# Prompt attention's scores, maxima and exponentials issued two turns ahead of the value products instead of one

## The chip, the cores and the metric

The kernel runs on one core of one Trainium2 chip. A core has five engines that work side by side, each with its own list of instructions and each waiting on semaphores for the others: TensorE (PE: matmuls, with its weight loads as PEld), VectorE (DVE), ScalarE (ACT), GpSimd (POOL, here mostly gathers by index) and SyncE (SP, which issues transfers). Matmul results land in PSUM banks and are read from there by DVE or ACT. The metric is the device time of one execution in microseconds (us); lower is better.

## The reference

One inference step of a hybrid decoder layer, for 512 prompt tokens and 8 samples of 4 new tokens each (their past is 4096 positions in a paged cache). The layer is a feed-forward block, a mixer of a gated linear recurrence (HGRN2, 4 heads) and a latent softmax attention (MLA, 4 heads), and a second feed-forward block:

```python
def layer(h, ...):
    h = h + 0.5 * rmsnorm(swiglu(rmsnorm(h, norm_g[0]), wg[0], wu[0], wd[0]), norm_g[1])
    m, c_kv, k_r, s_fin = mixer(rmsnorm(h, norm_g[2]), ...)
    h = h + rmsnorm(m, norm_g[3])
    h = h + 0.5 * rmsnorm(swiglu(rmsnorm(h, norm_g[4]), wg[1], wu[1], wd[1]), norm_g[5])

def mixer(u, ...):
    z = u @ w_in                        # columns for both head groups
    ...                                 # o_h: the recurrence's output
    qh = jnp.einsum('btc,chd->bthd', cq, w_q_up)
    ...                                 # rotary parts q_r, k_r; latent rows c_kv
    o_lat = mla_attend(q_lat, q_r, keys_c, keys_r, pos, k_pos)
    o_m = jnp.einsum('bthr,rhv->bthv', o_lat, w_uv)
    o = jnp.concatenate([o_h..., o_m...], axis=-1)
    return o @ w_out, c_kv, k_r, s_fin

def mla_attend(...):                    # per block of 128 queries
    s = (einsum('bqhr,bsr->bhqs', ql, c_kv) + einsum('bqhd,bsd->bhqs', qr, k_rope)) * scale
    s = jnp.where(k_pos <= q_pos, s, -jnp.inf)
    p = jax.nn.softmax(s, axis=-1)
    return einsum('bhqs,bsr->bqhr', p, c_kv)
```

## The kernel before

The 544 tokens are held with the features on the partitions and the tokens along the free axis, in two parts: part 0 is the prompt's first 256 tokens (tiles whose names end in a), part 1 the other 256 prompt tokens and the 32 sample tokens (names ending in b). Every large product is split in a high and a low part (`wh`/`wl`, `uha`/`ula`, `PTh`/`PTl`), three matmuls for one.

Around the change the program has these steps. A **turn** of the prompt attention is one pair (head, part); there are eight, `heads`: heads 0 to 3 of part 0, then heads 0 to 3 of part 1. A turn has these pieces.

- `prep(hd)`: the query projection of one head, 36 matmuls (line 259) on a weight tile split by ACT (`wh`, line 250) and DVE (`wl`, line 251), then scaled by DVE (lines 1158 to 1160) and split into `qnh` and `qnl`.
- `soft(hd, x)`: scores of two blocks of 128 queries on PE (lines 1188 and 1190), of 128 and 256 keys for part 0 and of 384 and 512 for part 1; the row maximum on DVE (1195, 1196), the exponential on ACT (1199), the division by the row sum on DVE (1200, 1201). The result is the tile `pe`.
- `latent(hd)`: the samples' latent query (1170, copied by ACT at 1171).
- `value(hd, x, pes)`: `pe` is transposed on PE (1211), split into `PTh` (ACT, 170) and `PTl` (DVE, 171), multiplied with the values (1220), and the sum `o` copied by ACT into `ma` or `mb` (1222).

The loop over turns is the code in which the changed number stands:

```python
PJ = (0, 0, 0, 0, 4, 4, 2, 1)
DP = 6
PJ0, LOOK = 4, 1
...
            for hd in range(LOOK):
                prep(hd)
            pe_ = [soft(*heads[i]) for i in range(LOOK)]
            for i, (hd, x) in enumerate(heads):
                if i + LOOK < len(heads):
                    if i + LOOK < NH:
                        prep(i + LOOK)
                    else:
                        qsplit_n(i + LOOK - NH, 1, qnb[:, i + LOOK - NH])
                    pe_.append(soft(*heads[i + LOOK]))
                ...
                value(hd, x, pe_[i])
```

From turn 4 (`PJ0`) on, the output projection of part 0, `project(0, ...)`, is woven in: eight products with `w_o` of 24 matmuls each, 4 in turn 4, 4 in turn 5; each is copied by ACT (770), squared (298), scaled (301), and the squares added by DVE (300). Its sum of squares `ssp` goes through PE (191) and two ACT steps (`rs_t` 197, `s_post` 198), and DVE then scales and adds (312, 313) before ACT and DVE split the second feed-forward block's input (207, 208). The first products of that block (line 277, steps of the generator `gb`) start there. `decode_prep` and `qsplit` copy the samples' queries into place (1229, 1231, 1238), and after the loop the sample decode begins, whose gathers (POOL, 1352 and 1359) use the slots of the prompt keys: `ulb`, `uhb`, `ha`, `hb`.

The written order isn't the executed one. A planner puts each engine's instructions in a fixed order; instructions that could go earlier are put between others, as long as data and buffers allow. PSUM tiles made with `ps(...)` come from four banks in rotation (`CYC`), so that a tile waits until the one made four before it has been read.

Of the kernel before, what the change touches and what calls it, by code (L numbers as in the profile page):

```python
# [47 lines left out]
PJ = (0, 0, 0, 0, 4, 4, 2, 1)  # L48
DP = 6
LAG, BEG = 2, 0  # L50
PJ0, LOOK = 4, 1
W1 = (5, 7)
NPS, PRT = {"ps": 2, "po": 1, "pm": 1, "acc": 4}, "ps"
CYC = ("ps", "po", "ps", "pm")
# [1640 lines left out]
```

## Time and profile before

| | |
|---|---|
| time of three runs | 1250.42 us median (1248.77 to 1251.25) |
| the profiled execution's own time | 1257.12 us |
| its span, first to last instruction | 1255.3 us |
| mean granted TensorE clock | 0.995 |
| PE busy | 1225.7 us (98%) |
| DVE, ACT, POOL busy | 983.8 us (78%), 742.0 us (59%), 72.4 us (6%) |
| moved by transfers | 195.59 MB, 156 GB/s |
| prompt attention and what is woven into it | from 619 to 703 us of the span |

The busy times are of one profiled execution. A group's line says how long its instructions took, not whether anything waited for them; that is read from the chain of waits (the work that ended last, followed back) and from the table of who waited for whom. Matmuls are pipelined: a matmul's duration is longer than the distance to the next one.

### The profile page before, as it was taken

To read this page: it belongs to the slowest core of one execution; us is meant where nothing else is said; L and a number is where in the kernel's file an instruction comes from. 1 tells how busy PE (TensorE), PEld (TensorE's weight loads), DVE (VectorE), ACT (ScalarE), POOL (GpSimd) and SP (SyncE) were. 2 spreads that over 40 slices of the span, in tenths; PEclk is the share of its full clock that TensorE was granted. 3 is DMA by queue.
4 is the path that set the end of the run, shared out by engine and by line. 5 is a ranking of instruction groups with operands and counts; after the bars stand their busy time and mean duration, and the time that the engine had idled before them with its cause. 6 is when DMAs were issued, how large, how long until landed. Compare 5 with 4: busy or idle time off the path is not lost.

```text
span 1255.3 us, 30001 instructions
## 1 busy us (share of the span) xinstructions
PE 1225.7 (98%) x12366; PEld 1157.1 (92%) x12366; DVE 983.8 (78%) x1976; ACT 742.0 (59%) x1559; POOL 72.4 (6%) x80
## 2 busy tenths in 40 slices
PE   8999999999999999999999899999999999999997
PEld 7999999999999988988889889878888999999997
DVE  7897788878679887877876899989987878466665
ACT  7675545544466655446668656665656777554454
POOL 0000000000000000000000412222310000000000
PEclk9999999999999999999999899999999999999999
DMA  6232333322164122324223959778776635645551
GB/s 236 85 118 87 100 101 101 94 96 94 51 227 158 60 89 69 104 77 148 75 92 118 374 178 347 292 249 299 252 273 218 204 104 191 188 137 182 145 160 59
DMA packets 73113, 195.59 MB, mean 156 GB/s; under 512 B 12336, under 2 KB 27728, under 8 KB 68240
## 3 DMA queue, kind: packets, MB, share of 16 engines
q1 hardware_dynamic: 64512, 150.47, 37.0%
q0 software_dynamic: 7168, 41.95, 9.2%
q8 instruction: 97, 1.59, 0.5%
q10 hardware_dynamic: 1296, 1.26, 0.3%
q14 instruction: 40, 0.33, 0.1%
HBM read 183.97 MB, written 9.67 MB: 154 GB/s over the span
## 4 chain that ended last, share of the span: by engine, by line
PE 86%; ACT 6%; DVE 5%; issue 2%; DMA 1%; SPq 0%; DVEq 0%; ACTq 0%
PE acc L259 29%; PE acc L277 18%; PE dn L259 8%; PE Y L561 6%; PE X L561 4%; PE Z L561 4%; PE s L1379 3%; PE acc L717 3%; PE o L1412 2%; ACT wh L250 1%; DVE wl L251 1%; PE pa L938 1%; ACT pbuf L1403 1%; PE acc L288 1%; PE zx L826 1%
## 5 line engine op out<-in xcount | busy, mean ns | idle before, releaser
L250 ACT CAST wh<-wraw 128x1024 fp32r<-128x1024 f32 (+2 forms) x194 | 185.3, 959 | 169.3 <-PE acc L259 108.6
L251 DVE TENSOR_TENSOR wl<-wraw,wh 128x1024 fp32r<-128x1024 f32 (+2 forms) x194 | 214.3, 1107 | 68.6 <-ACT wh L250 67.5
L277 PE MATMUL acc<-uha,wh 128*128 128x256 f32 (+1 forms) x528 | 155.7, 296 | 0.8 <-ACT uha L207 0.8
L277 PE MATMUL acc<-uha,wl 128*128 128x256 f32 (+1 forms) x528 | 150.6, 286 | 0.5 <-DVE wl L251 0.4
L277 PE MATMUL acc<-ula,wh 128*128 128x256 f32 (+1 forms) x528 | 150.9, 286 | 0.0
L259 PE MATMUL acc<-uhb,wh 128*128 128x288 f32 (+1 forms) x432 | 128.0, 296 | 0.0
L259 PE MATMUL acc<-uhb,wl 128*128 128x288 f32 (+1 forms) x432 | 127.0, 295 | 0.9 <-DVE wl L251 0.7
L259 PE MATMUL acc<-ulb,wh 128*128 128x288 f32 (+1 forms) x432 | 127.5, 295 | 0.0
L277 PEld LDWEIGHTS acc<-uha,wh 128*128 128x128 f32 x528 | 99.6, 189 | 8.8 <-issue 7.3
L277 PEld LDWEIGHTS acc<-uha,wl 128*128 128x128 f32 x528 | 99.5, 189 | 2.4 <-DVE wl L251 1.4
L277 PEld LDWEIGHTS acc<-ula,wh 128*128 128x128 f32 x528 | 99.8, 189 | 1.5 <-issue 1.2
L259 PEld LDWEIGHTS acc<-uhb,wl 128*128 128x128 f32 x432 | 81.2, 188 | 1.5 <-DVE wl L251 1.5
L259 PEld LDWEIGHTS acc<-uhb,wh 128*128 128x128 f32 x432 | 81.0, 188 | 0.2 <-ACT uhb L170 0.2
L259 PEld LDWEIGHTS acc<-ulb,wh 128*128 128x128 f32 x432 | 81.1, 188 | 0.1
L259 PE MATMUL dn<-hh,dh 128*128 128x272 f32 x256 | 74.3, 290 | 0.0
L259 PE MATMUL dn<-hh,dl 128*128 128x272 f32 x256 | 73.8, 288 | 0.0
L259 PE MATMUL dn<-hl,dh 128*128 128x272 f32 x256 | 73.6, 287 | 0.0
L1379 PE MATMUL s<-kh,q 64*32 64x128 f32 x2560 | 53.5, 273 | 5.3 <-issue 5.3
L277 PE MATMUL acc<-uhb,wh 128*128 128x272 f32 x176 | 52.8, 300 | 0.0
L1379 PEld LDWEIGHTS s<-kh,q 64*32 64x32 f32 x2560 | 38.5, 105 | 15.4 <-issue 10.5
L259 PE MATMUL acc<-hlb,wh 128*128 128x288 f32 x176 | 52.1, 298 | 0.0
L259 PE MATMUL acc<-hhb,wh 128*128 128x288 f32 x176 | 51.8, 298 | 0.0
(632 smaller groups left out, 3899.0 us busy)
## 6 DMA issues: line engine op xcount, KB each, us to landing
wraw<-w_u SPq DMA_DIRECT2D x66, 512.0 KB
wraw<-w_g SPq DMA_DIRECT2D x65, 512.0 KB
wraw<-w_d SPq DMA_DIRECT2D x40, 384.0 KB
wraw<-w_in SPq DMA_DIRECT2D x24, 512.0 KB
wraw<-w_d SPq DMA_DIRECT2D x32, 320.0 KB
wraw<-w_d SPq DMA_DIRECT2D x16, 512.0 KB
wraw<-w_o SPq DMA_DIRECT2D x16, 512.0 KB
g_S<-state SPq DMA_DIRECT2D x4, 512.0 KB
```

The costliest lines, as they stand in the source:

```text
L250: nc.scalar.copy(wh[:, :kt], w[:, :kt])
L251: nc.vector.tensor_tensor(wl[:, :kt], w[:, :kt], f32(wh[:, :kt]), op=ALU.subtract)
L259: nc.tensor.matmul(out, a, b, start=n == 0, stop=n == last)
L277: nc.tensor.matmul(acc[:, :n], a[:, k], b[:, k], start=k + i == 0, stop=k == kt - 1 and i == 2)
L288: nc.tensor.matmul(acc, a[:, k], b[:, k], start=k + i == 0, stop=k == kt - 1 and i == 2)
L561: nc.tensor.matmul(bank, a[p][:, k], b[q][:, k], start=first and k + n == 0, stop=k == 3 and n == 2, skip_group_check=True)
L717: nc.tensor.matmul(accs[x, d], wts[d][p][:, k], hs[k // 2][q][:, k % 2, x], start=k + n == 0, stop=k == nf - 1 and n == 2)
L826: nc.tensor.matmul(z, w[a][:, k], U[1][b][:, k], start=k + n == 0, stop=k == KD - 1 and n == 2)
L938: nc.tensor.matmul(po[es, c].rearrange("p (n m) -> p n m", m=m), kx[:, cs], up(qx[:, cs], m), start=True, stop=True, skip_group_check=True)
L1379: nc.tensor.matmul(self.s[r][c * 32 : c * 32 + 32, :P], q[rs, j], kh, start=st + jj == 0, stop=st == len(JS) - 1 and jj == 1, skip_group_c ...
L1403: (nc.scalar.copy if g else nc.vector.tensor_copy)(self.p[g * 32 : g * 32 + 32, c // 2, c % 2 * 4 : c % 2 * 4 + 4, self.i * 16 : self.i * ...
L1412: nc.tensor.matmul(o[g : g + 32, :R], self.p[:, c, a], self.craw[c][:, a], start=i + c == 0 and a < 4, stop=i + c == 2 and a >= 4, skip_gr ...
```

## The change

One number: `LOOK` goes from 1 to 2. Before the loop two heads are prepared and scored instead of one, and in turn i the scores, maximum and exponentials of turn i + 2 are issued instead of those of turn i + 1. Nothing is added or removed, and no tile gets another buffer (`pe` has three, `qnh`, `qnl`, `mx` and `sm` two each). The last two turns have no scores left to issue, where before it was the last one.

```diff
 LAG, BEG = 2, 0
-PJ0, LOOK = 4, 1
+PJ0, LOOK = 4, 2
 W1 = (5, 7)
```

The planner's order changes on PE, DVE, ACT and POOL; SP's stays. Three places show it; in the pieces of difference, names such as `q_8159` and `q_8192` are the same tile under another number.

ScalarE, in turns 2 to 4, where the first `w_o` products begin:

```order
-L1229 COPY q_8159<-qsT 32x128
 L1222 COPY ma<-o 128x256
-L1229 COPY q_8159<-qsT 32x128
+L1171 COPY qsT<-qa 128x64
+L170 CAST uha<-ma 128x256
+L170 CAST PTh<-tp 128x128
+L170 CAST PTh<-tp 128x2x128
+L1229 COPY q_8192<-qsT 32x128 x3
+L1199 ACTIVATE pe,sm<-s,mx 128x512
+L1229 COPY q_8192<-qsT 32x128 x6
+L1199 ACTIVATE pe,sm<-s,mx 128x384
+L1222 COPY ma<-o 128x256
```

The exponentials of the sixth and seventh turn and the copies of an attention output of part 0 now stand close together here; the exponential over 384 keys after the six copies is the seventh turn's, which stood behind the fourth `w_o` product before.

ScalarE, from the last `w_o` product (its copy is line 770) to the sum of squares:

```order
 L770 COPY ma<-acc 128x256
-L298 ACTIVATE sq_8589<-ma 128x256
+L170 CAST PTh<-tp 128x3x128
+L298 ACTIVATE sq_8622<-ma 128x256
+L170 CAST PTh<-tp 128x4x128
 L301 ACTIVATE ma<-ma,gv 128x256
-L170 CAST PTh<-tp 128x3x128
-L170 CAST PTh<-tp 128x4x128
-L1199 ACTIVATE pe,sm<-s,mx 128x384
-L1199 ACTIVATE pe,sm<-s,mx 128x512
-L1222 COPY mb<-o 128x256
 L197 ACTIVATE rs_t<-pr,epst 128x256
```

The last turn's two exponentials no longer stand between the two `PTh` casts and `rs_t`, and the copy `mb` goes behind `rs_t`.

TensorE, at the same place, just after the last `w_o` product:

```order
-L1188 MATMUL s<-hb,qr_7214 128x512
-L1190 LDWEIGHTS idb
-L1190 MATMUL s<-causb,idb 128x128
 L1211 MATMUL tp<-ident,pe 128x128 x7
 L1220 MATMUL o<-PTh,Vh 128x256
+L191 MATMUL pr<-ssp,ones 128x256
+L1211 MATMUL tp<-ident,pe 128x128 x3
 L1220 MATMUL o<-PTl,Vh 128x256
 L1220 MATMUL o<-PTh,Vl 128x256
```

The last turn's scores are gone from here (all fourteen rows of them; three are shown), and the sum of squares (`pr`) and three of the last turn's transposes go ahead of the seventh turn's value products instead of behind them.

## The prediction, made before the change was run

> **What bounds the kernel now.** I read the page's busy shares first, then the busy time by stretches, the table of PE's waits, and the chain of waits with the order of time of each engine around the change.
>
> ```profile
> PE 1225.7 (98%) x12366; PEld 1157.1 (92%) x12366; DVE 983.8 (78%) x1976; ACT 742.0 (59%) x1559; POOL 72.4 (6%) x80
> ```
>
> PE carries the kernel. The change adds no matmul, so the time can move only by PE's waits and by its clock. In the stretches (length, then busy time and count for PE, PEld, DVE, ACT and POOL, then granted clock, DMA share, GB/s) two places stand out inside the prompt attention:
>
> ```profile
> 650.00:660.00 10.00, 8.99 (x59) 7.00 (x58) 8.20 (x26) 8.61 (x27) 0.00 (x0) 1.00 0.07 29
> 660.00:670.00 10.00, 8.88 (x73) 8.47 (x72) 7.50 (x24) 9.70 (x24) 0.00 (x0) 1.00 0.19 56
> 690.00:700.00 10.00, 6.85 (x39) 5.54 (x38) 6.77 (x17) 5.36 (x14) 7.61 (x7) 0.83 0.85 340
> ```
>
> From 650 to 670 ACT is full (8.61 and 9.70 of 10) and PE loses about 1 us in each ten. From 690 to 700 nobody is full: PE is busy 6.85 of 10 and its clock falls to 0.83. The second is the end of the attention, and the chain of waits shows it as work handed from engine to engine:
>
> ```profile
> 687.93 0.88 PE s L1188 x5
> ...
> 688.88 1.21 PE s L1188 x5
> ...
> 690.53 1.02 ACT PTh L170 x2
> 691.56 0.58 ACT pe L1199 x2
> ...
> 692.38 0.61 DVE PTl L171
> ...
> 693.03 1.84 PE o L1220 x11
> 694.87 0.96 PE pr L191 x2
> ...
> 697.49 1.28 DVE ma L312 x2
> 698.77 1.20 DVE q L313 x2
> 699.98 0.61 DVE PTl L171
> ...
> 700.64 2.45 PE o L1220 x11
> 703.08 6.67 PE acc L277 x50
> ```
>
> The eighth and last `w_o` product ends where the last scores begin, 687.93; the dense stream of the next block begins at 703.08. I call these 15.15 us **the tail**. It should need only 2.1 us (0.88 + 1.21) for scores and a few for transposes and values; the rest is a sequence in which one engine waits for another.
>
> **The change, part by part.**
>
> *Front (turns 0 to 2).* Two heads are prepared and scored before anything else. At the end of the scores of the fourth turn, one head's latent query, transposes and values have not yet been done that were done before:
>
> ```profile
> 638.69 0.42 PE qa L1170 x4
> ...
> 639.50 0.41 PE tp L1211 x2
> ...
> 641.29 0.83 PE o L1220 x6
> ```
>
> That is 0.42 + 0.41 + 0.2 (the third transpose, half of the row for two) + 0.83 = 1.86 us of PE work that slides behind. One wait is new: DVE must finish the two softmaxes of both first turns before it scales the third head's query, and PE's third scores need it. A gain is excluded, since nothing that PE waits for comes sooner; I estimate 0.4 us, between 0 (PE has the third projection to work on meanwhile) and 1.2 (the longest wait for an exponential, first row of the table below), nearer to 0 as the projection covers most. So this stage ends 1.86 - 0.4 = 1.45 us earlier with 1.86 us of work owed.
>
> *Middle (turns 2 to 4), where ACT is full.* PE's waits from 618 to 760 us (what waited, for whom: us in total, times, longest) are
>
> ```profile
> PE o L1220 <- ACT pe L1199: 1.5, 2, 1.2
> PE acc L259 <- DVE wl L251: 0.8, 1, 0.8
> PE tp L1211 <- ACT ma L1222: 0.7, 1, 0.7
> ```
>
> and the last ACT step that PE waits for in this stretch is the cast of the fourth `w_o` tile, at 666.66. Ahead of it come, in addition, the copies of the head left over from the front and the exponentials of the seventh turn:
>
> ```profile
> 652.10 0.27 ACT ma L1222
> ...
> 653.12 0.30 ACT q L1229
> 653.45 0.37 ACT PTh L170
> ...
> 656.52 0.67 ACT pe L1199 x2
> ...
> 659.87 0.61 ACT pe L1199
> ...
> 666.66 1.06 ACT wh L250
> ```
>
> A head's copies run from 652.10 to 653.82, less the one foreign copy of 0.30: 1.4 us. The exponentials are 0.67 + 0.61 = 1.3. One `qsplit` copy (about 0.3, as the copy at 653.12) goes behind the cast. So ACT has 2.4 us more to do, starts 1.45 earlier, and the cast slips by 0.95 us; I take 1.2, since the transposes that waited 0.7 us for the copy `ma` now find that copy behind a further exponential. The bounds: if ACT had room for all of it, the slip is -1.45; if it starts no earlier, 2.4. Meanwhile PE does the seventh turn's scores (2.1 us) here, and from the fourth product on the order is as before, with the last turn's scores where the seventh's stood. The last `w_o` product therefore ends at 687.93 + 1.2 = 689.13, although 2.1 us more is done by then.
>
> *Tail.* Its pieces on ACT and DVE in their own order of time:
>
> ```profile
> 687.86 1.05 ACT L250 CAST wh<-wraw 128x1024 fp32r<-128x1024 f32 x1 [0.54 <-PE acc L259]
> 688.81 0.37 ACT L770 COPY ma<-acc 128x256 f32<-128x256 f32 x1
> 689.21 0.42 ACT L298 ACTIVATE sq<-ma 128x256 f32<-128x256 f32 x1
> ...
> 695.87 0.47 ACT L197 ACTIVATE rs_t<-pr,epst 128x256 f32<-128x256 f32 x1 [0.59 <-PE pr L191]
> ...
> 696.88 0.42 ACT L198 ACTIVATE s_post<-rs_t 128x256 f32<-128x256 f32 x1
> ```
>
> ```profile
> 690.53 0.42 DVE L300 TENSOR_TENSOR ssp<-ssp,sq 128x256 f32<-128x256 f32 x1
> ```
>
> Counted from the last product's end, with the planner's new order: the copy 770 starts at 0.88 (688.81, after the weight cast) and the step behind it at 1.28 (689.21); now that is a `PTh` cast (half of 1.02), then the square (0.42), finished at 2.2, then the second `PTh` cast, finished at 2.7. DVE adds the square by 2.2 + 0.42 = 2.6 and makes two `PTl` (0.61 each): 3.85. PE's sum `pr` can start at 2.7 behind the first value product and takes the 0.96 of now, until 3.7; three transposes; the other eleven value matmuls, 1.84 at the low clock, from about 4.1 to 5.9. From `pr` the chain goes on beside them: `rs_t` 0.47, a `PTh` cast 0.5, `s_post` 0.42 until 5.1; DVE's 1.28 and 1.20 until 7.6; the last `PTl` 0.61 until 8.2 (its `PTh` cast, after the copy of the eleven matmuls' result, is done by 7); eleven value matmuls, 2.45, until 10.6. There the stream begins: 10.6 us in place of 15.15. What went is the scores, the wait of the value product for the last turn's exponentials (the 1.2 us of the table) and the place of `pr` behind eleven value matmuls.
>
> *POOL.* The first four gathers need the prompt keys, so they follow the last scores:
>
> ```profile
> 689.69 1.91 POOL L1352 DMA_INDIRECT ulb<-pool_c,idx x1 [43.91 <-PE s L1188]
> ```
>
> They now go with the last scores to where the seventh turn's scores stood, plus the slip, about 675 (row below). I cost this at nothing: the transfers' share from 690 to 700 is 0.85 and falls, and a weight tile is issued five raw buffers (`wraw`) before its own cast. If that cover failed, four gathers of 1 MB at that row's 340 GB/s, an estimate of 12 us, would hold up a weight tile, and PE would wait at its cast. SP's order stays; two small gathers move behind a large one and have DVE's work of later steps as cover.
>
> *Sum.* 1.2 - (15.15 - 10.6) = -3.35 us. Everything behind 703 keeps its order on PE, ACT and DVE, and I let it shift as a whole. Against the profiled execution (1257.12 us with what lies around its span of 1255.3) that is 1253.8; that execution stands 6.7 above the median of the runs, to which I apply the same difference: 1250.42 - 3.35 = 1247.1.
>
> [...] The tail's low clock was taken from these stretches of two microseconds (columns as above):
>
> ```profile
> 694.00:696.00 2.00, 2.00 (x10) 1.71 (x9) 0.00 (x0) 0.51 (x2) 1.69 (x3) 0.50 0.98 401
> ...
> 702.00:704.00 2.00, 2.00 (x11) 2.00 (x11) 2.00 (x5) 0.93 (x3) 0.86 (x1) 0.50 0.98 408
> ```
>
> The clock is halved although the longest wait of PE before it was 1.2 us. [...] I keep the low clock in the sum.
>
> **The rivals.**
>
> *The clock stays up.* If the shorter tail keeps PE busy enough, its matmuls go at the full rate. Then the last eleven value matmuls take the time they have at full clock (second row; the first is the seventh turn's scores):
>
> ```profile
> 672.85 1.22 PE s L1188 x5
> ...
> 677.40 1.23 PE o L1220 x11
> ```
>
> The tail is 2.45 - 1.23 = 1.2 us shorter, and the stream's first microsecond, which now runs at 0.50 until about 704, gains 0.5: 1247.1 - 1.7 = 1245.4 us. For it: fewer us without work. Against: of the new tail's 10.6 us still some 5 are waits. [...]
>
> *Only the scores move.* If the sum of squares isn't reached sooner (say PE's first value product, ahead of it, waits for both `PTh` casts longer than I count), only the 2.1 us of scores leave the tail, and the slip of 1.2 takes half back: -0.9, 1249.5 us, no change that can be told. For it: the chain after `pr` (0.47, 0.42, 1.28, 1.20, 0.61, 2.45) is the same, in series. Against: in the new order two exponentials and eleven matmuls no longer stand ahead of `pr`.
>
> *ACT and DVE give it back (slower).* An exponential placed early waits for its maximum and holds the weight casts behind it. DVE's maximum over 512 keys of the seventh turn now stands behind eight `q` copies and a reciprocal that waits for the exponential before it:
>
> ```profile
> 645.87 0.22 DVE q L1231
> ```
>
> Eight of these are 1.8 us, 2 with the reciprocal. If these 2 us add to ACT's 2.4 with no earlier start, and the transposes' wait for `ma` grows from 0.7 to 2, the last product slips by 2.4 + 2 + 1.3 = 5.7, and the time is 1250.42 + 5.7 - 4.55 = 1251.6. It decides from a slip of 4.55 us on. For it: ACT's 9.70 of 10. Against: PE has `w_o` matmuls of three products to put in between.
>
> **How the numbers follow.** The forecast 0.50 (its own range 1244.5 to 1248.3, from the middle's bounds of -1.45 and 2.4), the clock staying up 0.13, only the scores 0.22, given back 0.15. A measurement of this kernel can tell about 0.2%, 2.5 us, from no change. Faster by more than that: over four fifths of the forecast and nearly all of the clock case, 0.54; slower: somewhat over half of the last case, whose waits may be longer than counted, 0.09; within: 0.37. The range that leaves two in ten out reaches from a little below the clock case, 1244.4, to the given-back case, 1251.4.
>
> **What the changed profile would show.** The cast of the fourth `w_o` tile about 1 us later; the last product's end near 689; no `s` between it and the transposes; `pr` some 3 us behind that end in place of 7; the stream beginning near 699.7; the gathers of `ulb` near 675; a second stretch at clock 0.50 still there. Wrong would be the forecast if the last product ended later than 692, if `pr` still came last, or if the decode behind took the 3 us back.

## The result, and the profile after

The changed kernel takes 1247.43 us (median of 22 runs, 1246.27 to 1250.05) against 1250.82 us for the kernel before on the same chip (22 runs, 1248.53 to 1252.14). The ratio is 0.9976 with a 95% interval of 0.9970 to 0.9982: 3.4 us faster. The forecast was 1247.1.

The engines of the whole execution say little (the page's first row, as for before):

```profile
PE 1217.1 (98%) x12366; PEld 1153.4 (93%) x12366; DVE 982.3 (79%) x1976; ACT 739.7 (59%) x1559; POOL 75.4 (6%) x80
```

The number of instructions is the same; PE is busy 8.6 us less. The spans of the two profiled executions, 1255.3 and 1246.1 us, differ by 9.2 us, far more than the medians do, and one has to see first what of this isn't the change. These rows are the samples' scores in the decode (2560 matmuls; the last numbers are the starts of the first and of the last one), of the kernel before, of the kernel before in a second execution, and of the changed kernel:

```profile
L1379 PE MATMUL s<-kh,q x2560: 266/269/294, 716.2 to 953.2; 64*32 64x128 f32 x197
```
```profile
L1379 PE MATMUL s<-kh,q x2560: 266/269/294, 716.0 to 947.2; 64*32 64x128 f32 x197
```
```profile
L1379 PE MATMUL s<-kh,q x2560: 266/269/294, 712.6 to 943.8; 64*32 64x128 f32 x197
```

The decode took 237.0, 231.2 and 231.2 us. So 5.8 of the 9.2 us belong to the execution that the prediction started from, not to the change; what can be the change's is the shift of 3.6 us (716.2 to 712.6; 3.4 against the second execution) with which the decode begins.

The stretches of the middle and of the end of the attention (length, busy time and count of PE, PEld, DVE, ACT, POOL, granted clock, DMA share, GB/s), after:

```profile
660.00:670.00 10.00, 9.20 (x73) 8.73 (x73) 7.80 (x22) 9.68 (x25) 0.00 (x0) 1.00 0.18 54
...
690.00:700.00 10.00, 7.68 (x48) 6.74 (x49) 9.21 (x17) 7.65 (x20) 3.04 (x3) 0.90 0.58 218
```

The middle is what it was: ACT 9.68 of 10 where it was 9.70. The end is denser: PE 7.68 of 10 in place of 6.85, 48 matmuls in place of 39. The chain of waits, from the fourth `w_o` tile to the stream (start, length, what):

```profile
667.89 1.06 ACT wh L250
...
679.82 9.20 PE acc L259 x77
689.05 0.47 ACT wh L250
...
690.00 0.37 ACT ma L770
690.37 0.38 ACT PTh L170
690.75 0.32 ACT sq L298
691.07 0.48 ACT PTh L170
691.59 0.38 PE o L1220
691.98 0.62 PE pr L191 x2
692.62 0.47 ACT rs_t L197
...
696.45 0.61 DVE PTl L171
697.11 1.90 PE o L1220 x11
699.01 7.22 PE acc L277 x50
```

No scores and no exponential stand in this chain; `pr` stands 2.9 us behind the last product's end (689.05), where it was 6.9 (694.87 less 687.93). The stream starts at 699.01 in place of 703.08. Of these 4.07 us, 0.29 were there before the attention began, as the same matmul of the key projection shows (before, then after):

```profile
600.63 0.29 PE L259 MATMUL acc<-q,wl 128*128 128x272 f32 x1
```
```profile
600.34 0.29 PE L259 MATMUL acc<-q,wl 128*128 128x272 f32 x1
```

That leaves 3.8 us: the last product ends 1.4 later (689.05 less 687.93, and 0.29), and the tail is 5.2 shorter. What the tail lost is seen by cutting it out of each profile (before, then after; here the cut after is at the first transpose, 688.97):

```profile
687.93:703.08 15.15, 11.85 (x63) 9.78 (x62) 10.93 (x24) 9.42 (x22) 7.92 (x7) 0.81 0.87 343
```
```profile
688.97:699.01 10.04, 7.62 (x52) 6.44 (x51) 8.22 (x15) 7.65 (x18) 2.11 (x2) 0.95 0.68 258
```

PE's idle time fell by only 0.9 us, from 3.30 to 2.42. Its busy time fell by 4.2, of which some 2.1 are the scores that now stand ahead of the cut; I put the other 2.1 us down to the same matmuls at a higher clock (0.95 in place of 0.81). So in these two executions the gain is one part order and one part clock, and the experiments had to part the two.

### The profile page after: what moved, and what is told of

It reads as the page before. It is cut to its first block, busy times and chain, and to the rows that moved or that the text cites. A ratio compares the mean times of both kernels' runs of the same rounds, so it can differ in the third digit from the quotient of the medians.

```text
span 1246.1 us, 30001 instructions
## 1 busy us (share of the span) xinstructions
PE 1217.1 (98%) x12366; PEld 1153.4 (93%) x12366; DVE 982.3 (79%) x1976; ACT 739.7 (59%) x1559; POOL 75.4 (6%) x80
## 4 chain that ended last, share of the span: by engine, by line
PE 79%; DVE 9%; ACT 8%; issue 2%; DMA 1%; SPq 0%; DVEq 0%; ACTq 0%
PE acc L259 29%; PE acc L277 14%; PE dn L259 8%; PE Y L561 7%; PE X L561 4%; PE Z L561 4%; PE acc L717 3%; DVE wl L251 2%; DVE kh L1367 2%; ACT pbuf L1403 2%; ACT wh L250 2%; PE s L1379 1%; PE pa L938 1%; PE s L1188 1%; PE o L1412 1%
## 5 line engine op out<-in xcount | busy, mean ns | idle before, releaser
L259 PE MATMUL acc<-hhb,wl 128*128 128x288 f32 x176 | 51.5, 295 | 0.0
L277 PE MATMUL acc<-uhb,wl 128*128 128x272 f32 x176 | 51.1, 290 | 0.0
```

What stands on the lines that cost most here:

```text
L259: nc.tensor.matmul(out, a, b, start=n == 0, stop=n == last)
L277: nc.tensor.matmul(acc[:, :n], a[:, k], b[:, k], start=k + i == 0, stop=k == kt - 1 and i == 2)
```

## The experiments

Ratios are to the kernel before on the same chip, with 95% intervals. In the first group (tail alone, front alone, gathers late, gaps filled) it took 1250.75 us, in the second (before once more, before with its gaps filled, both runs with eight products in turn 4) 1250.91; the third group, the last four runs, was on a chip on which it took 1257.72.

**The tail's order alone.** One turn ahead as before; only the last turn's scores come one turn sooner.

```diff
-                if i + LOOK < len(heads):
...
+                for j in ((i + 1,) if i < 5 else (6, 7) if i == 5 else ()):
...
+                    pe_.append(soft(*heads[j]))
```

> One turn ahead as before, but the last turn's scores are issued together with the seventh turn's, in turn 5. The front and the middle keep the order of before; from the last w_o product on TensorE has the order of the change. Theory (the gain is made in the tail): TensorE does 2.1 us more before the last w_o product, which ends near 690.0 in place of 687.93; the tail takes 10.0 us as in the changed kernel, the dense stream begins 3.0 us earlier, and the time is 1247.8 us. Rival (the gain comes from the two heads scored ahead at the front): no gain, 1250.8 us within 1.

Measured: 1248.11 us, ratio 0.9982 (0.9973 to 0.9991), 2.6 of the 3.4 us. Its profile is of the slowest of its eleven runs (1250.75 us). The last product ended 2.2 us later than in a second execution of before (689.88 and 687.66, from the rows under the kernel before once more), which is the scores' 2.1 and no more.

**The front's order alone.** Two turns ahead until turn 3, nothing issued in turn 4, one turn ahead again behind it.

```diff
+                for j in ((i + 2,) if i < 4 else (i + 1,) if 5 <= i < 7 else ()):
```

> Two turns ahead as in the change up to turn 3, nothing issued in turn 4, and one turn ahead again for the last two turns. The front has the order of the change, the tail that of before, scores included. Theory (tail): the tail keeps its 15.15 us; the front starts the middle 1.45 us earlier with 1.86 us owed and without the seventh turn's exponentials in it, so the sum is between -0.3 and +1.0: 1250.5 to 1251.8 us. Rival (front): most of the change's gain is here, 1247.0 to 1248.5 us.

Measured: 1250.83 us, ratio 1.0001 (0.9992 to 1.0010). The front by itself is worth nothing that can be told. Together the two runs put the gain into the tail, as far as intervals of 1 us each way allow.

**The kernel before once more.**

> The kernel before once more, unchanged, for a second profile and for what the measurement makes of no change. Theory: the profiled execution of before was one of the longer ones (1257.12 us against a median of 1250.4), and 5 of the 9.2 us between the two spans, which lie in the sample decode from 800 to 900 us of the span, are that execution's and not the change's; here the distance from the dense stream's start to the end of the span is that of the changed kernel, 547.1 us, within 1, the stream begins near 703, and the time is 1250.8 us. Rival: the change moves the decode too; then the distance is again near 552.

Measured: 1250.68 us, ratio 0.9999 (0.9990 to 1.0008), the decode of 231.2 us shown above, and 546.8 us from the stream's start to the end (547.1 in the changed kernel). The theory held. Of this kernel, of the front alone and of the tail alone, the chain shows the tail's two ends (where scores stand at the start, the last product ends there):

```profile
687.66 0.88 PE s L1188 x5
...
702.68 5.35 PE acc L277 x38
```
```profile
686.62 0.88 PE s L1188 x5
...
701.65 3.44 PE acc L277 x22
```
```profile
685.95 3.93 PE acc L259 x33
...
702.34 2.71 PE acc L277 x14
```

The tails are 15.0 us (before again), 15.0 (front alone) and 12.5 (tail alone: 685.95 + 3.93 to 702.34). The last has the changed kernel's order of TensorE from the last product on, and yet 12.5 us against 10.0. The tail of before again and of the tail alone, cut out as above:

```profile
687.66:702.68 15.02, 12.64 (x62) 10.56 (x62) 11.09 (x24) 9.39 (x22) 7.63 (x7) 0.71 0.83 316
```
```profile
689.88:702.34 12.46, 10.09 (x51) 8.90 (x50) 10.53 (x19) 7.53 (x18) 2.11 (x2) 0.67 0.49 177
```

PE is idle for 2.38 us in the one and for 2.37 in the other, as in the changed kernel (2.42). So at a clock as low as here the new order did not shorten PE's waits in sum. What the tail lost, 2.56 us, is mostly the scores, and they were paid for ahead of it: the stream began only 0.34 us earlier (702.34 and 702.68).

**The gathers late.** POOL waits for the seventh turn's `PTh` before the first four gathers.

```diff
+                if (hd, x) == (2, 1):
+                    late = mk([P, 4], F32, "late", pool=sb)
+                    for k, t in enumerate((Knl, Knh, Kh, Kl)):
+                        nc.gpsimd.tensor_tensor(late[:, k : k + 1], f32(t[:, 2, TP - 1 : TP]), f32(PTh[:, 0, P - 1 : P]), op=ALU.add)
```

> The changed kernel, with four one-column additions on POOL that read the prompt keys and the seventh turn's PTh, so that the first four gathers wait for that PTh and start near 691 in place of 675. Theory (the early gathers are worth nothing, as costed): 1247.4 us within 0.8, the same as the changed kernel. Rival (the gain is that transfers left the stretch from 690 to 700, where their share was 0.85 before): most of it goes, 1249.5 to 1251 us, and a weight cast waits for its transfer.

Measured: 1248.27 us, ratio 0.9979 (0.9970 to 0.9988). That is 0.87 us above the 1247.4 expected, just outside the 0.8 allowed, with an interval that holds the changed kernel's ratio of 0.9976. The first gather stood at 674.90 in the changed kernel and at 691.49 here (POOL's order of time):

```profile
674.90 1.91 POOL L1352 DMA_INDIRECT ulb<-pool_c,idx  x1 [31.41 <-PE s L1188]
```
```profile
691.49 1.12 POOL L1356 DMA_INDIRECT ulb<-pool_c,idx  x1 [0.17 <-DMA wraw<-w_u]
```

The rival's loss of 2 us or more is excluded; whether the sixteen microseconds by which the gathers come earlier are worth nothing or up to about 1 us is not settled. Its tail, with the same TensorE order again, was 12.5 us:

```profile
685.98 2.36 PE acc L259 x20
...
700.80 4.28 PE acc L277 x28
```

Why 12.5 and not 10.0 is read from one stretch of 14 us, cut alike from six executions: before, before again, the changed kernel, the tail alone, the gathers late, and the filled gaps, which come below. The clock is the third number from the end.

```profile
692.00:706.00 14.00, 11.76 (x63) 10.48 (x64) 10.77 (x25) 8.66 (x23) 8.50 (x7) 0.76 1.00 405
```
```profile
692.00:706.00 14.00, 12.87 (x65) 11.58 (x66) 11.02 (x25) 8.86 (x21) 7.77 (x7) 0.63 0.98 389
```
```profile
692.00:706.00 14.00, 13.27 (x91) 12.39 (x92) 12.71 (x28) 9.70 (x23) 4.68 (x3) 0.88 0.67 237
```
```profile
692.00:706.00 14.00, 12.88 (x66) 11.93 (x67) 11.53 (x24) 8.66 (x21) 2.09 (x2) 0.63 0.46 147
```
```profile
692.00:706.00 14.00, 13.32 (x76) 12.68 (x75) 11.44 (x26) 7.79 (x20) 8.39 (x7) 0.63 0.97 358
```
```profile
692.00:706.00 14.00, 13.72 (x107) 12.66 (x106) 13.33 (x30) 10.88 (x26) 4.42 (x3) 1.00 0.66 236
```

The low clock reads 0.50: from 698.1 to 701.4 us in the changed kernel, whose piece lies between 698.0 and 701.5, and in each stretch of 2 us from 696 to 704 in before again and in the tail alone. At 0.50 for h of 14 us the mean is 1 - h/28, so h is 6.7, 10.4, 3.4, 10.4, 10.4 and 0 us; I count these as none, one, two or three pieces of about 3.4, the length of the changed kernel's one. Before had 6.7 us in one execution and 10.4 in the other, with tails of 15.15 and 15.0. In these profiles the old tail hardly feels the clock; the new one does, 10.0 us with one piece and 12.5 with three. The starts of the stream say the same. Counted from the end of PE's last wait ahead of the attention's scores (615.91, 615.31, 615.91 and 614.97 us in the chains of waits), the stream begins after 86.8 us in before again, 86.3 in the front alone, 86.4 in the tail alone and 85.8 with the gathers late, all with three pieces; with one piece, it begins after 83.2 us in the changed kernel (699.01 less 615.82). With three pieces the whole new order (the gathers late stand for it) is worth some 0.9 us.

The pieces can be counted roughly in every run, profiled or not. In six profiles (before, changed, tail alone, front alone, gathers late, gaps filled), in stretches of 2 us up to 1244 us, the clock is below 1.00 only between 692 and 706 us and behind 1240. In these six, and in before again, the changed kernel once more, before with its gaps filled, the first run with eight products in turn 4 and the early sum of squares, the mean granted clock of the execution is 0.998 with no piece (1.00 from 692 to 706), 0.996 or 0.997 with one (0.88 there), 0.995 with two (0.76) and 0.994 with three (0.63); steps of 0.001 leave neighbours uncertain. Of the 22 runs of the changed kernel, six at 0.998 took 1246.3 to 1247.0 us, twelve at 0.996 or 0.997 took 1247.5 in the mean, and four at 0.994 took 1249.4 to 1250.1. Of the 29 runs of the kernel before in the first group, none is above 0.996: seven at 0.996 took 1249.6 in the mean, fourteen at 0.995 took 1250.7, eight at 0.994 took 1251.2. At an equal number of pieces the change is thus worth 2.2 us (one piece) or 1.5 (three); the rest of the 3.4 goes with fewer pieces, some 1.1 in the mean in place of 2.0. The runs of before do get shorter with fewer pieces, by 1.6 us, which its profiled tails do not show; whether the pieces make that time, or both follow from something else, is open.

**The gaps filled.** The changed kernel with idle matmuls (their result is overwritten) where TensorE waits in the tail.

```diff
                 o = ps("o")
+                for _ in range({6: 12, 7: 5}.get(x * NH + hd, 0)):
+                    nc.tensor.matmul(o[:, : 2 * P], Vh[:, 0, hd * P : (hd + 1) * P], Vh[:, 1, : 2 * P], start=True, stop=True, skip_group_check=True)
                 n = 0
```

> The changed kernel with 12 and 5 idle matmuls of 128x256 (their result is overwritten by the product behind them) in the two gaps of TensorE in the tail, of 1.70 and 0.67 us. Theory (the clock falls because work is broken): the granted clock stays at 1.00 from 689 to 702; the last eleven value matmuls take 1.24 us in place of 1.90, and the stream's first 2.3 us go at twice the rate, which is 1.15 us more: 1247.4 - 1.8 = 1245.6 us. Rival (the clock falls for another reason, or is decided elsewhere): a stretch of 3.4 us at 0.50 is still there, and the time is 1247.4 to 1247.9, as the idle matmuls overrun the gaps by a little.

Measured: 1247.67 us (7 runs, 1246.56 to 1248.11), ratio 0.9974 (0.9962 to 0.9985). In the profiled execution the clock is 1.00 from 692 to 706, PE's waits for other engines in the tail are down to 0.3 and 0.2 us, and the tail is 9.5 us. That the filling holds the clock up is not shown by this: three of the seven runs have a mean clock of 0.997, as with one piece, and six of the changed kernel's 22 runs have 0.998 without it. The expected 1.8 us are not there: 1245.6 would be 0.9959 of this group's before, below the interval. The four runs at 0.998 took 1246.6 to 1248.0 us, no less than the changed kernel's six. Whether the filled gaps save some tenths stays open.

**The kernel before with its gaps filled** (10 and 5 idle matmuls, the same lines).

> The kernel before with 10 and 5 idle matmuls of 128x256 (their result is overwritten by the product behind them) in its tail's gaps of 1.25 and 0.68 us; nothing else moves. Theory (broken work lowers the clock, and this is a part of what the change gained): the granted clock stays at 1.00 through the tail; the work that ran at half of it there (four value matmuls, the sum of squares and seven transposes, 1.5 us; eleven value matmuls, 1.2; the stream's first microsecond, 0.5) is 2 to 3 us shorter less what the idle matmuls overrun, so 1248.5 us, which would be two thirds of the change's gain without moving any score. Rival (the clock has no part, the scores alone): a half-clock stretch remains or nothing depends on it, 1250.8 within 0.6.

Measured: 1251.67 us, ratio 1.0007 (0.9998 to 1.0016): the theory's 1248.5 is refuted. The clock did rise, to a mean of 0.88 from 692 to 706 (one piece at half clock was left) where the second execution of before had 0.63, and nothing was saved. The profile says why in part: the idle matmuls need no data of the series, and yet they began late, since their PSUM bank came free only with the last turn's exponential,

```profile
PE o L1216 <- ACT pe L1199: 1.2, 1, 1.2
```

and so the value products behind them were pushed back. The sum of squares stood 7.1 us behind the last product (693.94 less 686.87) where it had stood 6.9 and 6.6 in the two executions of before; the tail was 14.6 us, 0.4 shorter, and that was lost again behind the stream's start (547.9 us to the end in place of 546.8). So the higher clock brought the old order nothing. That the wait for the exponential has to go first, as by moving the scores, is my reading of this and was not tested by itself.

**All eight `w_o` products in turn 4**, `PJ = (0, 0, 0, 0, 8, 0, 2, 1)`, and with the sum of squares one turn sooner, `(0, 0, 0, 0, 8, 2, 0, 1)`.

> The changed kernel with all eight w_o products issued in turn 4; the last turn's scores and the values of the sixth turn then go behind the last product, 4.3 us of TensorE work (2.1 + 0.8 + 1.35) that needs nothing of the sum of squares. Theory (the tail is a series through ScalarE and VectorE, and TensorE only has to be given work that is ready): the two gaps of 1.70 and 0.67 us are filled, 1247.4 - 2.4 = 1245.0, and up to 1.8 less where the clock stays up. Rival (work ahead of the sum of squares delays the series by as much): gaps come back between the sum of squares and the stream, 1247.4 to 1249.5.

> As the kernel with all eight w_o products in turn 4, with the sum of squares issued a turn earlier: it goes behind the seventh turn's last scores and the sixth turn's values, and ahead of eleven transposes and 24 value matmuls. Theory (what stands behind the sum of squares is what covers the series): this one is faster than the other order, about 1 us, 1244 to 1245 us. Rival (the series is delayed by the scores in either order): 1247.4 to 1249.5 us, as the other.

Measured: 1248.90 us, ratio 0.9986 (0.9977 to 0.9994), and 1250.66 us, ratio 0.9999 (0.9990 to 1.0008). Neither beats the change; both theories missed. In the first the scores stand directly ahead of the values again, and the old wait is back beside a later one (PE's waits from 686 to 790 us):

```profile
PE acc L288 <- ACT hha L170: 1.9, 1, 1.9
PE o L1220 <- ACT pe L1199: 1.3, 1, 1.3
```

More work that is ready did not help here, as it included scores whose exponential was then waited for.

**The changed kernel once more, and the sum of squares moved either way.** `PJ` is `(0, 0, 0, 0, 4, 4, 0, 3)` for late, `(…, 4, 5, 1, 1)` for early and `(…, 4, 5, 2, 0)` for early with the stream ahead of the last values.

> The changed kernel once more, unchanged, on the chip of the next three and for a second profile. Theory (the length of the half-clock stretch in the tail changes from execution to execution of one kernel, in steps of 3.41 us): 1247.5 us within 0.6; the stretch is 3.4, 6.8 or 10.2 us long, and the profile's tail goes with it, 10.0 us where it is 3.4 and about 12.5 where it is 10.2. Rival (the stretch belongs to the order of the instructions): again 3.41 us long, tail 10.0.

Measured: 1253.80 us (5 runs), ratio 0.9965 (0.9951 to 0.9978). The gain holds on a chip on which both kernels are slower (the five runs, at 0.996 to 0.998, do not show the order by clock seen above). The half clock had again one piece (0.88 from 692 to 706), but at 692 in place of 698, with a tail of 10.8 us: the first eleven value matmuls took 2.59 us there and the last eleven 1.23, so it also counts where the piece lies. Its decode took 237.3 us, as in the first profile of before.

> The changed kernel with the sum of squares issued behind the last turn's values: it goes behind all 24 value matmuls of both turns, as in the kernel before it stood behind eleven; the scores stay where the change put them. Theory (that the sum of squares comes ahead of the values is part of the gain): it stands some 6.5 us behind the last product in place of 2.9, nothing covers the 4.6 us from there to the first matmul of the stream, which begins at 11.3 in place of 10.0, and broken work lengthens the half clock: 1249.2 us (1248.4 to 1250.0). Rival (only the scores' move counts): 1247.4 us within 0.6.

Measured: 1259.98 us, ratio 1.0015 (1.0006 to 1.0024), some 6 us more than the changed kernel on this chip where 1.8 was expected. The direction is the theory's, the size is not:

```profile
688.75 0.02 issue
...
697.05 0.48 PE pr L191 x2
...
698.91 1.13 DVE wl L251
700.04 1.20 DVE ma L312 x2
...
703.50 5.86 PE acc L277 x34
```

`pr` came 8.3 us behind the last product, and on VectorE the decode's first maxima and a weight cast (1.13) went ahead of the scaling, so the stream began 14.8 us behind the last product in place of 10.8. That is 4 of the 6 us; the rest was lost later, in the decode, whose order moved too. So this run does not measure the place of the sum of squares alone.

> The changed kernel with the sum of squares issued in turn 5, directly behind the last product: it goes ahead of the seventh turn's first value product, behind three transposes, and ScalarE makes its two steps ahead of three PTh casts; the last eleven value matmuls stand behind twelve matmuls of the stream. Theory (the series from the sum of squares to the stream sets the tail's length): it stands 2.3 us behind the last product, the stream begins about 7 us behind it with 1.24 us of value matmuls still owed, so 10.0 - 7.0 - 1.3 = 1.7 us faster: 1245.7 us. Rival (VectorE, 9.2 of 10 busy here, is late with PTl and the splits instead): 1247.4 us or more, with TensorE waiting on VectorE in the stream's first microseconds.

> As the kernel with the early sum of squares, but its adding steps are issued in turn 6 too: 38 matmuls of the stream stand ahead of the last eleven value matmuls, and VectorE makes all scaling and adding before the last turn's PTl. Theory: the stream needs VectorE's scaled input first, so it runs without a break from about 7 us behind the last product, 1245.3 us. Rival (VectorE feeds the stream too slowly in either order): as the other, 1246 to 1247.5.

Measured: 1259.43 us, ratio 1.0009 (1.0000 to 1.0018), and 1257.19 us, ratio 0.9995 (0.9986 to 1.0004): both expectations missed, the gain of the change is gone. The first step failed at once (VectorE's order of time, then PE's waits, in the first of the two):

```profile
689.61 1.23 DVE L251 TENSOR_TENSOR wl<-wraw,wh 128x1024 fp32r<-128x1024 f32 x1 [1.28 <-ACT wh L250]
690.75 0.42 DVE L300 TENSOR_TENSOR ssp<-ssp,sq 128x256 f32<-128x256 f32 x1
```
```profile
PE pr L191 <- DVE ssp L300: 2.4, 1, 2.4
```

VectorE adds the last square only behind a weight cast of 1.23 us (the next step begins 1.14 us after it), so in this order of VectorE `pr` stands 2.8 us behind the last product (691.32 less 688.51) and not 2.3; ahead of the value product it makes PE wait 2.4 us in one piece. Most of the loss (the decode's scores end at 954.7 where they end at 948.8 in the changed kernel on this chip) lies behind the tail, in a decode in another order. That was not taken apart.

## Why the prediction held, point by point

*Front.* Said: 1.86 us of work slides behind, a new wait of 0.4 takes part of it, the stage ends 1.45 earlier. The same weight cast, before and after:

```profile
644.95 1.06 ACT L250 CAST wh<-wraw 128x1024 fp32r<-128x1024 f32 x1 [0.94 <-PE acc L259]
```
```profile
642.65 1.05 ACT L250 CAST wh<-wraw 128x1024 fp32r<-128x1024 f32 x1 [0.94 <-PE acc L259]
```

It is 2.30 earlier, 2.0 without the 0.29 of the start. The wait of 0.4 did not appear: in the chain the third scores follow the projection without a break,

```profile
630.51 4.55 PE acc L259 x36
635.07 0.51 PE s L1188 x5
```

so the estimate should have stood at its lower end, 0.

*Middle.* Said: the fourth cast slips by 0.95, the last product by 1.2. Measured: 667.89 against 666.66, 1.2, and with the 0.29 added 1.5; the last product 1.4. The wait of the transposes for `ma` grew from 0.7 to 1.0 (PE's waits after), as said:

```profile
PE o L1220 <- ACT PTh L170: 2.4, 2, 1.7
PE tp L1211 <- ACT ma L1222: 1.0, 1, 1.0
```

The early start and the later slip together are right to 0.2 us, but partly by luck. ACT's added work was read rightly: between the two casts just named (642.65 to 667.89, before 644.95 to 666.66) it was busy 21.59 us in place of 19.19, the 2.4 said. Its idle time there grew as well, from 2.52 to 3.65 us; the sum had only 0.25 for it, through the wait for `ma`. The 0.9 us missed there and the 0.55 by which the front came earlier than said have opposite signs.

*Tail.* Said: 15.15 to 10.6. Measured: 10.0 in one execution, 10.8 in the second, and 12.5 in the tail alone and with the gathers late, whose half clock was longer. The steps stand where they were put: `pr` at 2.9 ("some 3"), VectorE's last `PTl` done at 8.0 (8.2). The first row above is the gap that the ordering left, 1.7 us before the first value product.

*The clock in the tail.* This is the term that was wrong in kind; that the sum came out so close is luck, since the runs mix tails with none, one and three pieces. I took it as fixed at half for both groups of value matmuls (1.84 and 2.45 us); in the profile after, the first group stands before the half-clock piece (from 692.88 to 694.23) and only the second is slowed (1.90). In the profile after, the longest gap is 1.7 us, and the clock fell to 0.50 at 698.0. One piece stands at 698 in one execution of the changed kernel and at 692 in another, each of 3.4 us, so the point of change moves from run to run; what sets it is not shown. The rival "the clock stays up" (1245.4) is, by their mean clock, the case of the six runs at 0.998, which took 1246.6 in the mean: 0.9 us less than those with one piece, not 1.7. Its condition, that a busier TensorE keeps the full clock, was my guess; no run shows it. Where both groups do run at half clock, as in the tail alone (2.19 and 2.24 us in its chain of waits), the tail is 12.5 us and not 10.6. The sum left out what TensorE has to do between the two groups: four transposes (0.89), the decode's first scores (0.82 at full clock, 1.40 here), one value product (0.58) and two products of the stream (0.61). At half clock this takes longer than the series through VectorE that was followed: the last eleven value matmuls begin 10.2 us behind the last product in the tail alone (700.10 less 689.88) and 8.1 in the profile after (697.11 less 689.05). For the same reason "some 5" us of waits was too much; PE was idle for 2.4.

*POOL.* Said: about 675, worth nothing. Measured 674.90; with the gathers late the time was 0.8 us longer, no difference that can be told. No transfer stands in the changed kernel's chain of waits from the first gather to the stream.

*The other rivals.* "Only the scores move" is excluded by the chain (`pr` at 2.9); the late sum of squares, which turns the gain into a loss, points the same way, though its decode moved too. Its time, 1249.5, is nevertheless about what the four runs at 0.994 took (1249.4 to 1250.1), and its 0.9 us what the order is worth above with three pieces: with a long half clock little more than the scores' move is left of the gain. "Given back" is excluded by the slip of 1.4 us, where it decides from 4.55.

*The starting point.* The prediction put its sum against one execution and carried its distance to the median, 6.7 us, unchanged. The second profile of before bears this out: 5.8 of it are the decode of that execution.

## What to carry to other kernels

Where a stage ends in a series that hops from engine to engine, issue ahead of it everything that another engine must still work on, an exponential above all. The busiest engine's own work is only moved by that (the scores were paid for ahead of the tail); what was gained here is a tail that was shorter where the clock was up (10.0 us with one piece at 0.50, 12.5 with three), which the old one, held by the series, was not in its profiles (15.15 with two, 15.0 with three). More ready work or another place for the sum of squares did not add to the change, as they left or brought back a wait of the series; filling the gaps took the waits away and still gained nothing that can be told. Before two profiles are subtracted, read the granted clock of every run, find a landmark behind the change and check with a second profile that what follows it is equal.

## What the hardware showed that was not expected

The time at half clock from 692 to 706 us was 0, 3.4, 6.7 or 10.4 us in the six executions cut there (a mean clock of 1.00, 0.88, 0.76 or 0.63) and differed between executions of one kernel (before: 6.7 and 10.4; under the changed TensorE order of the tail: 3.4, 3.4, 10.4 and 10.4). In the new tail that is worth 2.5 us (10.0 against 12.5), which is of the size of the spread of its 22 runs, 3.8 us. Run by run the granted clock goes with it: the six runs at 0.998 are all shorter than 1247.0 us, the four at 0.994 all longer than 1249.3. What decides in which execution the clock falls for how long was not found. On the chip of the last group the decode took 237.3 us in place of 231.2, with the same instructions; why is open.
